# Batched matrix product on one core: two groups stored between loads, the rest in three transfers, and eight blocks of the last half copied by VectorE

## The chip, the core and the metric

The kernel runs on one core of one Trainium2 chip. The metric is the device time of one execution in microseconds; before the change it was 132.04 us, the median of three runs (131.92 to 132.06). The engines named below are TensorE (PE, with its weight loads as PEld), VectorE (DVE), ScalarE (ACT), GpSimd (POOL) and SyncE (SP), which here computes nothing and issues all transfers.

## What is computed

```python
def setup_inputs():
    batch, dim_i, dim_j, dim_k = 32, 256, 512, 384
    return {
        "x": np.random.randn(batch, dim_i, dim_j).astype(np.float32),
        "y": np.random.randn(batch, dim_j, dim_k).astype(np.float32),
    }

def reference(x: np.ndarray, y: np.ndarray) -> np.ndarray:
    return np.einsum('bij,bjk->bik', x, y).astype(np.float32)
```

These are 32 products of a 256 x 512 matrix with a 512 x 384 matrix in float32. Read from DRAM are 41.94 MB, written are 12.58 MB.

## The kernel before

The 32 batches are cut into N = 8 groups of Q = 4. Each batch of a group has a quarter of the 128 partitions (PQ = 32). A group's x is one load of 2048 KB, its y one load of 3072 KB; x and y each have two buffers, so group n uses the buffers of group n − 2. The result of every group has its own place in `o_sb`, which holds the whole output, 1536 KB for each group; no store has to be finished before a buffer can be used again.

A group is worked in two halves (NE = 2, the loop over `e`), each with half of the rows of x. For each group GpSimd rounds x to float16 (`round_x`, one cast for each half) and y (`round_y`, two casts of 128 x 3072, or four of 128 x 1536 in groups 0, 6 and 7). VectorE transposes x in blocks of 32 x 32, four pieces for each half (`transpose_x`). TensorE makes 64 small products for each half, in four chunks of 16 (NC = 4); a chunk waits for its piece of y and of transposed x. The products add up in the PSUM banks of the half; two halves have different banks.

A half's result is 16 blocks of 32 x 384 (`BLOCKS`, in order of bank g and row block h). They are copied from PSUM to `o_sb` by two engines: the last five (`OWN = 5`) by VectorE, at the end of `vector_half`, the other eleven by ScalarE, in `scalar_half`, which waits for each bank in turn. In the last half of the last group VectorE first waits until all of its matmuls are done, and then copies its five; it has no more transposes by then. Both engines raise a semaphore at the end of each half (`s_act`, `s_dve`). TensorE takes one from each before a half starts. So when the first chunk of a group's second half is done, both halves of the group before it have been copied. The stores rest on that.

SyncE's program sets the order of all transfers. Ahead of it stand the loads of groups 0 and 1 (y, x, x, y). Then, for n from 2 to 7, x of group n is issued when GpSimd has rounded both halves of x of group n − 2, and y of group n when the first half of x of group n − 1 is rounded, which GpSimd does only after y of group n − 2. The first store, of groups 0 to 5 (`JOINED = 6`), is issued behind all loads, when the first chunk of the second half of group 6 is done. The second, of groups 6 and 7, is issued when the copies of the last half are finished. SyncE then waits for both to land. All of these transfers go through one queue, in the order in which they are issued, spread over the 16 DMA engines. In DRAM and in `o_sb`, each partition's part of a group is one run of 12,288 bytes, whatever number of groups a store has.

Names for the steps below: `chunk_done(n, e, a)` is the count of `s_pe` at which chunk a of half e of group n is done; `s_cast` counts the rounded halves of x; `store(first, last)` is one transfer of the groups from `first` up to, but without, `last`.

Of the kernel before, what the change touches and what calls it, by code (L numbers as in the profile page):

```python
# [11 lines left out]
Q = 4  # L12
NE = 2
STEP = 4
STRAIGHT = 2
JOINED = 6


@with_exitstack
def kernel(  # L20
# [13 lines left out]
    H = R // NE  # L34
    T = J // PQ
    TW = T // 2
    N = B // Q
# [20 lines left out]
    s_act = nc.alloc_semaphore("s_act")  # L58
    s_dve = nc.alloc_semaphore("s_dve")
    s_pe = nc.alloc_semaphore("s_pe")  # L60
    s_sp = nc.alloc_semaphore("s_sp")
    s_out = nc.alloc_semaphore("s_out")
    mine = s_x + s_y + [s_xt, s_yr, s_cast, s_free, s_act, s_dve, s_pe, s_sp]
# [3 lines left out]
    def load_x(n):  # L67
        src = x[n * Q : (n + 1) * Q].rearrange("g (p r) j -> (g p) r j", r=R)
        return nc.sync.dma_start(out=x_sb[n % 2], in_=src).then_inc(s_x[n], 16)

    def load_y(n):
        src = y[n * Q : (n + 1) * Q].rearrange("g (q t) k -> (g q) t k", t=T)
        return nc.sync.dma_start(out=y_sb[n % 2], in_=src).then_inc(s_y[n], 16)
# [11 lines left out]
    def bank_done(n, e, g):  # L85
        return (n * NE + e) * MARKS + NC + g

    def chunk_done(n, e, a):
        return (n * NE + e) * MARKS + (a + 1 if a < NC - 1 else MARKS)

    sp = nc.sync

    def store(first, last):
        groups = out[first * Q : last * Q].rearrange("(n g) (s f) k -> (g s) n f k", g=Q, s=PQ)
        src = o_sb[:, first:last].rearrange("p n e h k -> p n (e h) k")
        sp.dma_start(out=groups, in_=src).then_inc(s_out, 16)

    for n in range(2, N):
        sp.wait_ge(s_cast, NE * (n - 1))
        load_x(n)  # L100
        sp.wait_ge(s_cast, NE * (n - 1) + 1)
        load_y(n)
    sp.wait_ge(s_pe, chunk_done(JOINED, NE - 1, 0))
    store(0, JOINED)
    sp.wait_ge(s_pe, chunk_done(N - 1, NE - 1, 0))
    sp.drain()
    sp.wait_ge(s_act, NE)
    sp.wait_ge(s_dve, NE)
    store(JOINED, N)
    sp.sem_inc(s_sp, 1)  # L110
    sp.wait_op(s_out, 16 * 2, "sem-ge").then_inc(s_out, -16 * 2)

# [34 lines left out]
    v = nc.vector  # L149
# [4 lines left out]
    def transpose_x(e, a):  # L154
        w = slice(a * AW, (a + 1) * AW)
        v.transpose(xt_w[:, w], words[:, e, w]).then_inc(s_xt, 1)  # L156

    BLOCKS = [(g, h) for g in range(Q) for h in range(H)]  # L160
    OWN = 5

    def collect(copy, n, e, blocks, first=None, last=None):
        for i, (g, h) in enumerate(blocks):
            ins = copy(  # L165
                o_sb[g * PQ : (g + 1) * PQ, n, e, h],
                o_ps[h * PQ : (h + 1) * PQ, e * Q + g, :K],
            )
            if i == 0 and first is not None:
                ins.then_inc(first, 1)  # L170
            if i == len(blocks) - 1 and last is not None:
                ins.then_inc(last, 1)

    def vector_half(n, e):
        for a in range(NC):
# [3 lines left out]
            transpose_x(1 - e, a)  # L179
        collect(v.tensor_copy, n, e, BLOCKS[-OWN:], s_free, s_dve)  # L180

# [6 lines left out]
            vector_half(n, e)  # L188
    vector_half(N - 1, 0)
    v.wait_ge(s_pe, chunk_done(N - 1, 1, NC - 1))  # L190
    collect(v.tensor_copy, N - 1, 1, BLOCKS[-OWN:], None, s_dve)

    a_ = nc.scalar

    def scalar_half(n, e):
        for g in range(Q - 1):
            a_.wait_ge(s_pe, bank_done(n, e, g))
            blocks = [b for b in BLOCKS[:-OWN] if b[0] == g]
            collect(a_.copy, n, e, blocks, None, s_act if g == Q - 2 else None)


    a_.copy(spare, nc.const_aps.tensor(0.0, [1, 1], F32))  # L202
    a_.sem_inc(s_act, NE)
    with a_.Fori(0, N - STRAIGHT) as n:
        with a_.Fori(0, NE) as e:
            scalar_half(n, e)
    for n in range(N - STRAIGHT, N):
        for e in range(NE):
            scalar_half(n, e)

    te = nc.tensor

# [68 lines left out]
```

## Time and profile before

| | |
|---|---|
| median of 3 runs | 132.04 us |
| the profiled execution, its own time | 132.04 us |
| its span (first to last instruction) | 130.7 us |
| outside the span | 1.34 us |
| granted TensorE clock, mean | 0.831 |
| TensorE matmul busy | 64.1 us (49%) |
| VectorE busy | 82.5 us (63%) |
| ScalarE busy | 84.3 us (64%) |
| GpSimd busy | 74.1 us (57%) |
| moved by DMA | 54.55 MB, mean 417 GB/s |

All times of the profile are in microseconds from the start of the span, unless marked ns. A row of the timeline has the start, the duration, the engine, the line, the operation with its output and input, and how many instructions of the kind were merged into the row; in brackets stands how long the engine was idle before, and who ended that. A row of a transfer has the output and input, the issuing queue, the count, the size and the time from issue to landing; where one issue is wanted, the view was limited to a window that holds it alone. A row of the windows has the stretch, its length, the busy time and the count for PE, PEld, DVE, ACT and POOL, then the granted TensorE clock, the busy share of the 16 DMA engines, and GB/s.

### The profile page before, as it was taken

The page shows a single profiled execution, that of the slowest core. Times are in us where ns is not written, and L with a number is a line of the kernel's source. Part 1 is how long each engine was busy: PE and PEld are TensorE (multiplying, and loading weights), DVE is VectorE, ACT ScalarE, POOL GpSimd, SP SyncE. Part 2 cuts the span into 40 slices and gives each one's busy share as a digit, 9 for nine tenths or more (in the row PEclk, how much of TensorE's full clock was granted, in tenths as well). Part 3 has the DMA queues.
Part 4 walks back from the last instruction along what each step waited for, and adds up shares of the span by engine and source line. Part 5 has one row for each costly group of instructions (what it writes and reads, how often), then busy time and mean ns, then how long its engine had stood idle before and what let it go on. Part 6 is the DMA issues. An engine that isn't in the chain of part 4 may idle for free. (4 is left out here: it accounts for less than half of the span.)

```text
span 130.7 us, 3199 instructions
## 1 busy us (share of the span) xinstructions
PE 64.1 (49%) x1024; PEld 48.7 (37%) x1024; DVE 82.5 (63%) x144; ACT 84.3 (64%) x178; POOL 74.1 (57%) x42
## 2 busy tenths in 40 slices
PE   0000009950797199369909945892684498100000
PEld 0000009930796086169805524761252255000000
DVE  0000036599549998996999799899979959900000
ACT  0400000399809997996999699899989958993000
POOL 0006991089946993995599399757973970000000
PEclk9999999999559959955896897799999869955555
DMA  5999999999999999999999999999999999999995
GB/s 128 451 399 451 411 451 429 466 399 446 414 434 406 456 421 416 441 439 429 431 444 399 451 406 469 399 416 436 474 399 400 432 427 429 440 425 421 432 432 244
DMA packets 3363, 54.55 MB, mean 417 GB/s; under 512 B 288, under 2 KB 288, under 8 KB 288
## 3 DMA queue, kind: packets, MB, share of 16 engines
q1 hardware_dynamic: 3360, 54.53, 98.1%
q14 instruction: 3, 0.02, 0.0%
HBM read 41.94 MB, written 12.58 MB: 417 GB/s over the span
## 5 line engine op out<-in xcount | busy, mean ns | idle before, releaser
L165 ACT COPY o_sb<-o_ps (+1 forms) x176 | 82.8, 470 | 30.9 <-PE o_ps L217 28.8
L217 PE MATMUL o_ps<-y_r,xt_sb 32*128 32x384 f16 x1024 | 64.1, 393 | 47.6 <-PEq L214 47.5
L217 PEld LDWEIGHTS o_ps<-y_r,xt_sb 32*128 32x128 f16 x1024 | 48.7, 110 | 62.6 <-issue 54.4
L156 DVE STREAM_TRANSPOSE xt_sb<-x_r 128x256 f32<-128x256 f32 x64 | 37.9, 624 | 30.5 <-POOL x_r L126 18.4
L136 POOL CAST y_r<-y_sb 128x1536 f16<-128x1536 f32 (+1 forms) x22 | 44.3, 2050 | 13.8 <-DMA y_sb<-in_y_dram 13.8
L165 DVE COPY o_sb<-o_ps 32x384 f32 (+1 forms) x80 | 44.6, 557 | 1.6
L126 POOL CAST x_r<-x_sb 128x2048 f16<-128x2048 f32 x16 | 30.2, 1896 | 18.9 <-DVE o_sb L165 16.0
L202 ACT ACT_TABLE_LOAD x1 | 1.3, 1283 | 3.5 <-PEq L78 3.5
L265 POOL MEMSET const-float32-0.0<- 128x1 f32 x1 | 0.1, 98 | 0.2 <-issue 0.2
L202 ACT COPY spare<-const-float32-0.0 1x1 f32<-1x1 f32 x1 | 0.2, 190 | 0.0
L265 POOL MEMSET const-uint8-127<- 128x1 uint8 x1 | 0.1, 102 | 0.0
L265 POOL MEMSET const-bfloat16-1.0<- 128x1 bf16 x1 | 0.1, 101 | 0.0
L265 POOL MEMSET const-float32-1.0<- 128x1 f32 x1 | 0.1, 99 | 0.0
## 6 DMA issues: line engine op xcount, KB each, us to landing
y_sb<-in_y_dram SPq DMA_DIRECT2D x8, 3072.0 KB, 15.5
x_sb<-in_x_dram SPq DMA_DIRECT2D x8, 2048.0 KB, 15.4
out_dram<-o_sb SPq DMA_DIRECT2D x1, 9216.0 KB, 26.0
out_dram<-o_sb SPq DMA_DIRECT2D x1, 3072.0 KB, 12.0
```

Of the source, the lines that this page charges most:

```text
L126: po.tensor_copy(x_r[:, e], x_sb[n % 2][:, e * H : (e + 1) * H]).then_inc(s_cast, 1)
L136: ins = po.tensor_copy(y_r[:, s], y_sb[n % 2][:, s])
L156: v.transpose(xt_w[:, w], words[:, e, w]).then_inc(s_xt, 1)
L165: ins = copy(o_sb[g * PQ : (g + 1) * PQ, n, e, h], o_ps[h * PQ : (h + 1) * PQ, e * Q + g, :K],)
L202: a_.copy(spare, nc.const_aps.tensor(0.0, [1, 1], F32))
L217: return te.add_instruction(mybir.InstMatmult(name=nc.get_next_instruction_name(), start_tensor_calc=start, stop_tensor_calc=stop, tile_si ...
L265: nc = _bacc.Bacc("TRN2", target_bir_lowering=False, num_devices=1)
```

## The change

SyncE issues the store of groups 0 and 1 between the loads of x and y of group 5 (`BEHIND = 5`), behind a wait for the first chunk of the second half of group 2. The rest of the output goes in three transfers in place of two: groups 2 to 5, where the store of groups 0 to 5 was; group 6, when the first chunk of the second half of group 7 is done; and group 7, when the last copies are finished. The drain of SyncE ahead of the last waits is gone, and the final wait counts four stores.

In the last half of the last group, VectorE copies the last 8 of the 16 blocks (`LAST_OWN = 2 * H`, H = 4) and ScalarE the first 8, those of banks 0 and 1. All other halves stay at 5 and 11.

```diff
+EARLY = 2
+BEHIND = 5
 JOINED = 6
...
     for n in range(2, N):
         sp.wait_ge(s_cast, NE * (n - 1))
         load_x(n)
+        if n == BEHIND:
+            sp.wait_ge(s_pe, chunk_done(EARLY, NE - 1, 0))
+            store(0, EARLY)
         sp.wait_ge(s_cast, NE * (n - 1) + 1)
         load_y(n)
     sp.wait_ge(s_pe, chunk_done(JOINED, NE - 1, 0))
-    store(0, JOINED)
+    store(EARLY, JOINED)
     sp.wait_ge(s_pe, chunk_done(N - 1, NE - 1, 0))
-    sp.drain()
+    store(JOINED, N - 1)
     sp.wait_ge(s_act, NE)
     sp.wait_ge(s_dve, NE)
-    store(JOINED, N)
+    store(N - 1, N)
     sp.sem_inc(s_sp, 1)
-    sp.wait_op(s_out, 16 * 2, "sem-ge").then_inc(s_out, -16 * 2)
+    sp.wait_op(s_out, 16 * 4, "sem-ge").then_inc(s_out, -16 * 4)
...
     OWN = 5
+    LAST_OWN = 2 * H
...
-    collect(v.tensor_copy, N - 1, 1, BLOCKS[-OWN:], None, s_dve)
+    collect(v.tensor_copy, N - 1, 1, BLOCKS[-LAST_OWN:], None, s_dve)
...
-    def scalar_half(n, e):
-        for g in range(Q - 1):
+    def scalar_half(n, e, own=OWN):
+        mine = BLOCKS[:-own]
+        for g in range(mine[-1][0] + 1):
             a_.wait_ge(s_pe, bank_done(n, e, g))
-            blocks = [b for b in BLOCKS[:-OWN] if b[0] == g]
-            collect(a_.copy, n, e, blocks, None, s_act if g == Q - 2 else None)
+            blocks = [b for b in mine if b[0] == g]
+            collect(a_.copy, n, e, blocks, None, s_act if g == mine[-1][0] else None)
...
-            scalar_half(n, e)
+            scalar_half(n, e, LAST_OWN if (n, e) == (N - 1, NE - 1) else OWN)
```

## Prediction

> **What bounds the kernel now.** I read the page first, then SyncE's order of issues, then how long each transfer took to land, then the last 30 us.
>
> ```profile
> span 130.7 us, 3199 instructions
> ...
> DMA  5999999999999999999999999999999999999995
> ...
> q1 hardware_dynamic: 3360, 54.53, 98.1%
> ...
> ACT o_sb L165 8%; PE o_ps L217 4%
> ```
>
> The second row is the mean busy share of the 16 DMA engines in 40 slices: nine tenths or more in every slice but the first and the last. The third row is the one queue through which all loads and stores go: 54.53 MB, and its packets take 98.1% of the span of 16 engines. The last row is the chain of waits; it covers only 12% of the span, and ends in ScalarE's copies, after which only the last store is left. So the bound is the bytes in the queue, and the kernel can lose or gain only where the queue stands empty, or where a transfer has a price beside its bytes. The bytes are the same before and after.
>
> SyncE's issues (start, duration, line, count):
>
> ```profile
> 0.74 0.39 SPq L73 DMA_DIRECT2D y_sb<-in_y_dram  x1
> ...
> 53.42 0.33 SPq L69 DMA_DIRECT2D x_sb<-in_x_dram  x1
> 60.65 0.33 SPq L73 DMA_DIRECT2D y_sb<-in_y_dram  x1
> ...
> 76.85 0.33 SPq L69 DMA_DIRECT2D x_sb<-in_x_dram  x1
> 84.08 0.33 SPq L73 DMA_DIRECT2D y_sb<-in_y_dram  x1
> 97.43 21.69 SPq L96 DMA_DIRECT2D out_dram<-o_sb  x2
> ```
>
> These are y of group 0, x and y of group 5, x and y of group 7, and the two stores (97.43, and the second at 118.72, quoted below). From issue to landing, in the same order, for y of group 0, x and y of group 7 and the stores of six groups and of two:
>
> ```profile
> y_sb<-in_y_dram SPq DMA_DIRECT2D x1, 3072.0 KB, 10.1
> x_sb<-in_x_dram SPq DMA_DIRECT2D x1, 2048.0 KB, 16.9
> y_sb<-in_y_dram SPq DMA_DIRECT2D x1, 3072.0 KB, 17.1
> out_dram<-o_sb SPq DMA_DIRECT2D x1, 9216.0 KB, 26.0
> out_dram<-o_sb SPq DMA_DIRECT2D x1, 3072.0 KB, 12.0
> ```
>
> Issue plus this time gives the landings: x of group 7 at 93.75, its y at 101.18, the first store at 123.43, the second at 130.72, which is the end of the span. The second store was issued 4.7 us before the first one had landed, so it waited in the queue and never let it run dry: it landed 7.29 us behind the first. **7.3 us is what two groups' store costs in a full queue**, 3.65 us for one group.
>
> **The store of groups 0 and 1.** Its wait is for the first chunk of the second half of group 2.
>
> ```profile
> 50.31 2.78 PEld L217 LDWEIGHTS o_ps<-y_r,xt_sb 32*128 32x128 f16 x64 [0.53 <-issue]
> ...
> 76.78 5.44 POOL L136 CAST y_r<-y_sb 128x3072 f16<-128x3072 f32 x2
> ...
> 82.16 1.90 POOL L126 CAST x_r<-x_sb 128x2048 f16<-128x2048 f32 x1
> ```
>
> TensorE loads the 64 weights of that half from 50.31 on, in four chunks, so the first chunk is over around 51; SyncE comes to the wait at 53.42 + 0.33 = 53.75 and finds it met. Queued behind it on SyncE is y of group 5, which is issued at 60.65 in any case, since it waits for a cast: nothing is late there, and the added 0.4 us of issuing is hidden in that wait (were the cover gone, it would delay y by those 0.4 us, in a queue that holds over 10 us of work).
>
> In the queue the store stands ahead of y of group 5. That y, and all transfers behind it, land 7.3 us later. Does the queue run dry later for that? The issue most at risk is y of group 7, which waits for GpSimd's cast of x of group 6, behind the cast of y of group 5. That cast of y begins at 76.78 now, right when y lands, and at 84.1 then; it takes 5.44, the x cast 1.90, so y of group 7 is issued at 91.4. x of group 7 ahead of it lands at 93.75 + 7.3 = 101.05. The cover is 9.7 us. The queue stays full, and all work from group 5 on is 7.3 us later: y of group 7 lands at 108.5. The price of the store is the time that it no longer takes at the end: zero in the sum.
>
> **Two more transfers, two more turns.** There are four stores for two, and the queue turns once more from reading DRAM to writing it, and once from writing to reading. The first store's 9216 KB took 123.43 − 101.18 = 22.25 us, against 3 × 7.29 = 21.87 for three times the second store, which has three transfers' worth of fixed cost in it: a boundary in a full queue shows no price. The 0.38 us over may be a turn to writing, or engines that end at different times. Bounds: nothing below (no byte is saved), 0.38 for a turn to writing. A turn from writing to reading has no row; its ends are nothing and the price of a load that finds the queue empty. That was paid by y of group 0: with its first packets at 1.75 (row below) it landed at 10.84, 9.09 us for 3072 KB against 7.29, so 1.8 us. The rows nearest to a turn in a full queue are those of stores behind loads, so I take **0.2 us for all of it** and keep 0 to 2.2.
>
> The Trainium skill, in "DMA: Bandwidth & Descriptors", section "Anatomy of one DMA — SWDGE (gpsimd) path", speaks against this change: every DMA has a fixed cost of about 2.0 us whatever its size, most of it for confirming the last write. Two more in series would be 4 us by that. The rows agree for a transfer that finds the queue empty (1.8 us), and not for one in a full queue.
>
> **The tail.** Copies of the last group (start, duration, engine, count), the matmuls of its halves, and the last issue:
>
> ```profile
> 103.21 4.87 PE L217 MATMUL o_ps<-y_r,xt_sb 32*128 32x384 f16 x64 [3.87 <-PEq L214]
> ...
> 108.10 10.60 ACT L165 COPY o_sb<-o_ps 32x384 f32<-32x384 f32 x22 [1.74 <-PE o_ps L217]
> ...
> 108.48 3.21 PE L217 MATMUL o_ps<-y_r,xt_sb 32*128 32x384 f16 x64 [0.40 <-PEq L214]
> 108.86 5.73 DVE L165 COPY o_sb<-o_ps 32x384 f32<-32x384 f32 x10
> 118.72 0.39 SPq L96 DMA_DIRECT2D out_dram<-o_sb  x1
> ```
>
> ScalarE makes 22 copies in 10.60 us, 0.482 each, and ends at 118.70; VectorE makes 10 in 5.73, 0.573 each. With 8 blocks each in the last half, ScalarE makes 11 + 8 = 19 copies and ends at 108.10 + 9.16 = 117.26. VectorE ends its first five at 111.73, just behind the last matmul (111.69), and eight more at 116.31. ScalarE is still the later, and the last store can be issued 1.44 us earlier: at 118.72 − 1.44 + 7.3 = **124.58**. Before, these 1.44 us would have been hidden, for the queue was full until 123.43; now they count. Without them the issue would be at 126.02.
>
> When does the queue run dry? Quarters of a microsecond, DMA share and GB/s at the end of the row; a packet counts where it starts:
>
> ```profile
> 1.75:2.00 0.25, 0.00 (x0) 0.00 (x0) 0.00 (x0) 0.00 (x0) 0.00 (x0) 1.00 4.66 1081
> ...
> 128.75:129.00 0.25, 0.00 (x0) 0.00 (x0) 0.00 (x0) 0.00 (x0) 0.00 (x0) 0.50 1.27 541
> ...
> 129.75:130.00 0.25, 0.00 (x0) 0.00 (x0) 0.00 (x0) 0.00 (x0) 0.00 (x0) 0.50 0.12 49
> ```
>
> The first engines start their last packet before 129.0, the last one at 129.75 or later: they end raggedly, over about 1 us. One group's store earlier, and with the 0.2 us, they run out of group 6's store from about 125.5 on. The last store's packets start about 1.0 us behind its issue (0.74 to 1.75 for the first load): 125.6. The two meet. If the queue is never dry, the span is 130.7 + 0.2 = 130.9. If the store starts cold, it ends at 124.58 + 1.0 + 3.65 + 1.8 = 131.05. The later one holds: **131.05**, or 0.35 over the span before. The two issues of 0.39 us ahead of it (groups 2 to 5, and 6) are made while SyncE waits for the copies, and the removed drain is worth nothing that a row shows.
>
> The sum: 0 for the moved store, 0.2 for boundaries and turns, 0.15 for the cold start beside them; with the 1.34 us that lie outside the span (132.04 less 130.7) the profiled execution becomes 132.39. It equals the median of the runs shown, so I forecast **132.4 us**. About 0.2%, or 0.26 us, is what a measurement here can tell from no change.
>
> **Rivals.** (a) *Nothing shows, the not-slower side*: boundaries and turns cost nothing and the last store arrives in time: 132.0 to 132.2. For it: no boundary shows a price in the rows. It decides as soon as the store is issued about 0.2 us earlier, or a store's start, which reads on-chip memory, costs less than the first load's 1.8.
>
> (b) *The tail is late.* TensorE's clock (the number ahead of the DMA share) changes within the last group:
>
> ```profile
> 106.00:107.00 1.00, 1.00 (x17) 0.55 (x9) 0.64 (x1) 0.36 (x1) 0.96 (x1) 0.50 1.03 426
> 107.00:108.00 1.00, 1.00 (x21) 0.39 (x16) 0.55 (x1) 0.00 (x0) 0.00 (x0) 0.94 1.04 442
> ```
>
> Its first half ran mostly at half clock (4.87 us), the second at full (3.21). Shifted by 7.3 us, the second half can fall in a stretch at half clock and take 1.66 us more; VectorE, which waits for all of it, would start at 113.35 and end at 117.93, past ScalarE's 117.26, and a slow last chunk of the first half adds some 0.4. The store is then up to 1.1 us later, and so is the end: 132.8 to 133.5. A first half at full clock gains little, as the casts feed it. (c) *A turn from writing to reading costs like a cold load*, 1.8 us, and everything behind it, the last store too, moves: 131.05 + 1.8 + 1.34 = 134.2. Against it: the next loads already stand in the queue. (d) *Each added transfer pays its price in series*, 2 × 1.8: 135.6; the second store's 7.29 us speaks against it. (e) *Faster*: the ragged end shrinks, as the last transfer is half as long, and the engines end together near 129.5 instead of past 130: 131.5. No row shows a reason.
>
> **How the numbers follow.** Forecast 0.38, (a) 0.30, (b) 0.16, (c) 0.06, (d) 0.02, (e) 0.08. The range from 131.8 to 133.4 holds the forecast, (a), nearly all of (b) and a part of (e). The forecast lies 0.36 over the time before, just past what can be told apart, so 0.31 of its 0.38 count as slower; with (b), (c) and (d) that makes 0.55. Same: 0.07 of it and most of (a), 0.36. Faster: 0.09.
>
> **What would show it.** y of group 5 landing 7.3 us later, near 84; y of group 7 issued near 91 and the queue still full then; y of group 7 landing near 108.5, where later means a turn's price; ScalarE's last run with 19 copies; the last issue near 124.6, and whether the DMA share dips around 125.5. A dip of over 1 us makes (b), none makes (a). A queue that is empty anywhere between 60 and 108 would make the argument wrong.

## The result, and the profile after

| | before | after |
|---|---|---|
| median | 132.06 us (6 runs, 131.92 to 132.14) | 133.23 us (6 runs, 132.96 to 133.34) |
| ratio, with its 95% interval | | 1.0086 (1.0073 to 1.0099) |
| the profiled execution, its own time | 132.04 us | 133.21 us |
| its span | 130.7 us | 131.8 us |

The change makes the kernel 1.17 us slower. From the page after:

```profile
span 131.8 us, 3200 instructions
...
DMA  5999999999999999998999999999999999999994
...
q1 hardware_dynamic: 3392, 54.53, 97.6%
...
ACT o_sb L172 7%; PE o_ps L225 1%
```

The bytes are the same, and the 16 DMA engines are as busy as before in nearly every slice. 97.6% of 131.8 is 128.6 us of packets, against 98.1% of 130.7 = 128.2 before: the mean engine works 0.4 us longer for the same bytes, and the span is 1.1 us longer. SyncE's issues after, and then the landings of y of group 0, the early store, y of groups 5 and 7, the store of groups 2 to 5 and the last store, each from its issue:

```profile
53.78 0.33 SPq L71 DMA_DIRECT2D x_sb<-in_x_dram  x1
54.16 0.43 SPq L98 DMA_DIRECT2D out_dram<-o_sb  x1
61.01 0.34 SPq L75 DMA_DIRECT2D y_sb<-in_y_dram  x1
...
77.22 0.33 SPq L71 DMA_DIRECT2D x_sb<-in_x_dram  x1
92.03 0.33 SPq L75 DMA_DIRECT2D y_sb<-in_y_dram  x1
106.19 19.36 SPq L98 DMA_DIRECT2D out_dram<-o_sb  x3
```

```profile
y_sb<-in_y_dram SPq DMA_DIRECT2D x1, 3072.0 KB, 10.4
out_dram<-o_sb SPq DMA_DIRECT2D x1, 3072.0 KB, 23.2
y_sb<-in_y_dram SPq DMA_DIRECT2D x1, 3072.0 KB, 23.6
y_sb<-in_y_dram SPq DMA_DIRECT2D x1, 3072.0 KB, 17.1
out_dram<-o_sb SPq DMA_DIRECT2D x1, 6144.0 KB, 18.2
out_dram<-o_sb SPq DMA_DIRECT2D x1, 1536.0 KB, 6.6
```

The early store is issued right behind x of group 5, without a wait, and lands at 77.36; y of group 5 lands at 84.61, y of group 7 at 109.13 (101.18 before), groups 2 to 5 at 124.39. The last issue ends at 106.19 + 19.36 = 125.55, so it begins at 125.16, and lands 6.6 us later, at 131.8. The tail's timeline after:

```profile
111.11 3.87 PE L225 MATMUL o_ps<-y_r,xt_sb 32*128 32x384 f16 x48 [3.00 <-PEq L222]
...
116.03 9.16 ACT L172 COPY o_sb<-o_ps 32x384 f32<-32x384 f32 x19 [1.11 <-PE o_ps L225]
...
116.46 3.17 PE L225 MATMUL o_ps<-y_r,xt_sb 32*128 32x384 f16 x64 [0.43 <-PEq L222]
116.80 7.42 DVE L172 COPY o_sb<-o_ps 32x384 f32<-32x384 f32 x13
```

The copies stand as in the sum: 19 in 9.16 us on ScalarE, which ends at 125.19, and VectorE before it, at 124.22. How the engines end, by the share of all 16 that is busy (second last column), in the kernel before and then after:

```profile
129.00:130.00 1.00, 0.00 (x0) 0.00 (x0) 0.00 (x0) 0.00 (x0) 0.00 (x0) 0.50 0.27 111
130.00:130.70 0.70, 0.00 (x0) 0.00 (x0) 0.00 (x0) 0.00 (x0) 0.00 (x0) 0.50 0.00 0
```

```profile
129.00:130.00 1.00, 0.00 (x0) 0.00 (x0) 0.00 (x0) 0.00 (x0) 0.00 (x0) 0.50 0.87 369
130.00:131.80 1.80, 0.00 (x0) 0.00 (x0) 0.00 (x0) 0.00 (x0) 0.00 (x0) 0.50 0.07 27
```

In the last 1.8 us after, a share of 0.07 is 2.0 us of work, about what one engine does. The trace has 16 landings for each transfer, one for each engine's part, and the end is the last of them: here fifteen parts of the last store landed from 130.14 to 131.10, and the sixteenth at 131.81. The page's busy share, a mean of 16, does not show that one.

### The profile page after: what moved, and what is told of

The parts are those of the page before. It is cut to its first block, busy times and chain, and to the rows that moved or that the text cites. A ratio compares the mean times of both kernels' runs of the same rounds, so it can differ in the third digit from the quotient of the medians.

```text
span 131.8 us, 3200 instructions
## 1 busy us (share of the span) xinstructions
PE 65.6 (50%) x1024; PEld 53.1 (40%) x1024; DVE 84.1 (64%) x147; ACT 82.8 (63%) x175; POOL 74.1 (56%) x42
## 3 DMA queue, kind: packets, MB, share of 16 engines
q1 hardware_dynamic: 3392, 54.53, 97.6%
## 5 line engine op out<-in xcount | busy, mean ns | idle before, releaser
L172 ACT COPY o_sb<-o_ps (+1 forms) x173 | 81.4, 470 | 38.7 <-PE o_ps L225 36.7
L225 PE MATMUL o_ps<-y_r,xt_sb 32*128 32x384 f16 x1024 | 65.6, 407 | 54.0 <-PEq L222 50.6
L225 PEld LDWEIGHTS o_ps<-y_r,xt_sb 32*128 32x128 f16 x1024 | 53.1, 113 | 66.2 <-issue 59.3
L172 DVE COPY o_sb<-o_ps 32x384 f32 (+1 forms) x83 | 46.2, 557 | 1.7
```

The source lines that it names most:

```text
L172: ins = copy(o_sb[g * PQ : (g + 1) * PQ, n, e, h], o_ps[h * PQ : (h + 1) * PQ, e * Q + g, :K],)
L225: return te.add_instruction(mybir.InstMatmult(name=nc.get_next_instruction_name(), start_tensor_calc=start, stop_tensor_calc=stop, tile_si ...
```

## The experiments

Two things were read from the trace's packet records in every run. A store's packet of 12,288 bytes takes 460 ns where nothing disturbs it. The records do not name the engine; packets of which each starts where the one before it ends are taken for one engine's. In the kernel before, there is such a run of some 16 packets, with 484 to 549 ns each, beside the matmuls of the last group. And in most kernels with an early store there is a stretch of 2 to 3 us in which loads' packets on all 16 engines take longer. The table has, for each profiled execution: the sum of what the slow store packets of one engine (about 478 ns and more) take over 460 ns, ahead of the last load (early) and beside group 7's matmuls or later (late), the time that slow loads cost per engine (their excess over 912 or 611 ns, divided by 16), the mean and the last of the 16 landings of the last transfer, all in us. Packets of under 12 KB are not in its first two columns, nor are those slowed by more than 180 ns that start where an instruction load of 8 KB ends (in the kernel before, one of 698 ns at 100.89, where a load begun at 100.58 had taken 309 ns). As engines are told apart by times alone, the late column is good to about 0.1 us.

```
kernel            early  late  loads  mean end  last end   time of this execution
before             0     0.79  0       129.86    130.68    132.04
before_again       0     0.79  0       129.87    130.44    131.84
no_early           0     0.89  0.01    129.88    130.49    131.85
tiny_early         0     0.79  0.13    129.90    130.74    132.13
pe_on              0     2.48  0       129.97    132.31    133.68
one_before_x       0     0.86  0.44    130.26    131.04    132.44
one_early          0.33  0.78  0.39    130.19    131.42    132.82
four_turns         -     0.81  0.50    130.28    131.26    132.62
four_together      -     0.87  0.41    130.56    131.52    132.89
store_before_x     0.36  0.84  0.44    130.89    131.53    132.89
two_gaps           0.02  0.87  0.56    131.13    131.34    132.70
after              0.84  0.80  0.44    130.56    131.81    133.21
after_again        0.73  0.85  0.38    130.41    131.70    133.10
own5_last          0.84  0.77  0.53    132.12    132.19    133.56
```

The late column is some 0.8 us in every kernel but `pe_on`, with an early store or without.

Three theories stood at the start: the last store meets a drained queue (1), the turns between loads and stores and the further transfers cost (2), and the engine that ends last carries delays of its own (3). The expectations below add two: 3a, matmuls slow one engine's stores, and 4, having an early store at all is what costs.

**Parts of the change alone.** `no_early` takes the early store out:

```diff
-        if n == BEHIND:
-            sp.wait_ge(s_pe, chunk_done(EARLY, NE - 1, 0))
-            store(0, EARLY)
...
-    store(EARLY, JOINED)
+    store(0, JOINED)
```

> The early store is taken out; groups 0 to 5, 6 and 7 go in three transfers at the end, and VectorE copies 8 of the last 16 blocks. Theory 1: the last copies are done near 117.3 and the queue is full until about 127, so 132.0 to 132.2. Theory 2: one boundary more than before and no turn back to reading, so 132.0 to 132.3. Theory 3: 132.0 to 133.0, by how late the first load lands and what hits the last engine.

Measured: 132.00 us, ratio to before 0.9998 (0.9982 to 1.0014). The split of the end, one transfer more, VectorE's eight blocks and the missing drain neither cost nor save together, within that interval of about 0.2 us. The 1.17 us come with the early store.

`one_early` stores only group 0 there, with `EARLY = 1`:

> Only group 0 is stored between x and y of group 5; groups 1 to 5, 6 and 7 in three transfers at the end. The last copies are then 3.65 us earlier against the same end of the queue, so the last store finds the queue full. Dry queue at the end (theory 1): nearly all of the 1.17 us is gone, 132.1 to 132.4. Turn between stores and loads, and the number of transfers (theory 2): the turns and transfers are the same as in the changed kernel, so it stays at 132.9 to 133.3. Slowest engine (theory 3: the engines start and end raggedly, and the one that ends last carries delays from the start and from other packets on it, which differ from program to program): anywhere between 132.0 and 133.2, with a first load that lands later than 10.84 us in step with the time.

Measured: 132.62 us, 1.0037 (1.0019 to 1.0056), about half of the loss for half of the bytes. That is above what a drained queue alone would leave and below what turns would. It lies in the wide range of theory 3, but the sign named there failed: the first load's landing did not follow the time (10.98 us for the last of its 16 parts, 11.14 in the changed kernel, 10.99 in `before_again`).

`own5_last` gives ScalarE its 11 blocks back:

```diff
-    LAST_OWN = 2 * H
+    LAST_OWN = OWN
```

> The changed kernel, but VectorE copies 5 of the last 16 blocks again and ScalarE 11. The last issue is 1.44 us later, near 126.6. Theory 1: the queue is already drained at the last store, so the end moves by the full 1.4 us, to 134.5 to 134.8. Theories 2 and 3: the last store still had some cover on the engine that ends last; the end moves by less, 133.6 to 134.3.

Measured: 133.51 us, 1.0103 (1.0066 to 1.0139), some 0.2 to 0.3 us above the changed kernel, where the drained queue wanted 1.4, and 0.1 below the least that the other theories had expected. So the drained queue is not what the changed kernel pays. The last column but one of the table says how: here all engines end within 0.07 us of their mean (132.12 and 132.19). The last issue, 106.01 + 21.47 − 0.39 = 127.09, is 1.93 us later than in the changed kernel, and the end 0.38: the slowest engine had some 1.5 us of older work left in the changed kernel's execution.

```profile
106.01 21.47 SPq L98 DMA_DIRECT2D out_dram<-o_sb  x3
```

`before_again` is the kernel before, unchanged:

> The kernel before, unchanged, for a second profile: by all theories 132.0 to 132.2. Under theory 3 the landing of the first load and the ragged end may differ from the first profile's 10.84 and 0.9 us, and the time with them.

Measured: 131.84 us. Its first load lands at 10.99, later than the 10.79 of the first profile by the same event, and its time is shorter: in this pair, how raggedly the engines start is not what sets the time.

**Matmuls beside stores.** `pe_on` is the kernel before, with matmuls added that compute nothing for the output:

```diff
+    te.wait_ge(s_act, 1)
+    te.wait_ge(s_dve, 1)
+    with te.Fori(0, 20):
+        for t in range(4):
+            for g in range(Q):
+                s = slice(g * PQ, (g + 1) * PQ)
+                product(o_ps[:, g, K:512], xt[s, t // 2, :, t % 2], y_r[s, t, :512 - K], True, True, g)
+    product(o_ps[:, 0, K:512], xt[:PQ, 0, :, 0], y_r[:PQ, 0, :512 - K], True, True, 0).then_inc(s_pe, 1)
```

> The kernel before, with 321 more small matmuls (128 columns each, into unused columns of PSUM, read by nothing) behind the last half, so that TensorE goes on working while the last stores run. In the packet records of before, one of the 16 DMA engines takes 484 to 549 ns for each of 16 packets in a row where the others take 460, and that stretch (103.8 to 111.8) is the one in which TensorE works on the last group. If stores that run beside matmuls are slowed on one engine (theory 3a), that engine goes on losing some 45 ns a packet for 20 to 30 packets more: 132.6 to 133.5. If turns and transfers, or a drained queue, are the cost (theories 1 and 2): 131.9 to 132.2.

Measured: 133.43 us, 1.0106 (1.0089 to 1.0123). The only wait for them stands on SyncE behind the last store's issue, and they end at 122.87, long before that store lands; the queue has the same transfers. From its timeline and its windows:

```profile
113.91 8.96 PE L218 MATMUL o_ps<-y_r,xt_sb 32*128 32x128 f16 x321 [2.24 <-ACT o_sb L166]
```

```profile
103.20:112.00 8.80, 8.27 (x128) 4.22 (x128) 6.41 (x12) 6.42 (x15) 3.75 (x3) 0.81 1.01 427
112.00:113.90 1.90, 0.00 (x0) 0.02 (x1) 1.83 (x5) 1.84 (x5) 0.00 (x0) 1.00 0.98 420
113.90:123.00 9.10, 8.50 (x321) 5.61 (x321) 1.10 (x2) 5.07 (x11) 0.00 (x0) 0.81 1.01 427
123.00:129.00 6.00, 0.00 (x0) 0.00 (x0) 0.00 (x0) 0.00 (x0) 0.00 (x0) 0.68 1.00 428
129.00:130.00 1.00, 0.00 (x0) 0.00 (x0) 0.00 (x0) 0.00 (x0) 0.00 (x0) 0.50 0.32 135
130.00:132.30 2.30, 0.00 (x0) 0.00 (x0) 0.00 (x0) 0.00 (x0) 0.00 (x0) 0.50 0.05 21
```

Fifteen engines are done by 130.35, much as before; 0.05 of 16 engines over 2.3 us is 1.8 us of one engine that works on alone. The slow packets' start and duration (us, ns), beside them:

```
103.85 512  104.35 501  104.85 493  105.34 512  106.30 507  107.28 493  107.76 502  108.26 521
108.78 484  109.26 521  109.78 531  110.31 559  110.85 521  111.37 512
114.17 568  114.74 578  115.31 540  115.85 578  116.41 578  116.98 568  117.53 568  118.09 568
118.65 596  119.24 578  119.81 540  120.35 531  120.88 587  121.46 568  122.02 549  122.57 568  123.13 493
```

They stop where TensorE pauses (111.9 to 113.9), though VectorE and ScalarE go on copying there, and where it ends. That TensorE's work slows the stores of one DMA engine is shown: the slow stretch came and went with the matmuls, and the end moved with it. How it does so is not shown. The loads that ran beside matmuls earlier in the same trace have no such packets.

`store_before_x`, `one_before_x` and `two_gaps` move early stores into TensorE's pauses. The first puts the changed kernel's early store ahead of x of group 5:

```diff
-        load_x(n)
         if n == BEHIND:
             sp.wait_ge(s_pe, chunk_done(EARLY, NE - 1, 0))
             store(0, EARLY)
+        load_x(n)
```

> The changed kernel, with the early store ahead of x of group 5 in place of behind it, so that about half of it runs where TensorE is idle between groups 3 and 4. Theory 3a (matmuls beside a store slow one engine): the delay of that engine halves, 132.6 to 133.0. Theory 2 (turns): the same turns, 133.1 to 133.4. Theory 1 (drained queue): the end of the queue and the last copies stand as in the changed kernel, 133.1 to 133.4.

Measured: 132.86 us, 1.0059 (1.0043 to 1.0076). The slow engine's early part fell from 0.84 to 0.36 us (0.73 in `after_again`), and the time by 0.37, as the theory of the matmuls has it; the intervals of the two ratios only just meet. Here the mean engine did wait for the last store (it landed 4.18 us behind the one before, where a full queue takes 3.65), but the last engine did not (131.53 − 127.88 = 3.65).

`one_before_x` does the same with `EARLY = 1`:

> Only group 0 is stored early, ahead of x of group 5, in TensorE's pause. one_early, where it stands behind that x and beside matmuls, had 132.62. Theory 3a: only a stall of all engines once in the run, 0.2 to 0.4 us, remains: 132.2 to 132.45. Without an effect of matmuls: 132.5 to 132.7, as one_early.

Measured: 132.62 us, 1.0045 (1.0004 to 1.0087), four runs from 132.27 to 133.51, as spread as the runs of before beside them (131.74 to 132.78). By its time alone it tells nothing apart. By its packets it does: none of the early store's is slow (0 against 0.33 us in `one_early`), and the last engine of the profiled execution ends 0.38 us earlier.

`two_gaps` stores groups 0 and 1 one by one, each in a pause:

```diff
-        load_x(n)
-        if n == BEHIND:
+        if BEHIND <= n < BEHIND + EARLY:
             sp.wait_ge(s_pe, chunk_done(EARLY, NE - 1, 0))
-            store(0, EARLY)
+            store(n - BEHIND, n - BEHIND + 1)
+        load_x(n)
```

> Groups 0 and 1 are both stored early, as in the changed kernel, but one ahead of x of group 5 and one ahead of x of group 6, where each falls mostly into TensorE's pause between two groups. One transfer and one turn more than the changed kernel, the same bytes early, the same end. Theory 3a (matmuls slow one engine's stores): that engine loses little beside the early stores, and the time falls by 0.5 to 0.8 us, to 132.4 to 132.8. Theory 2 (turns): 133.3 to 133.6. Theory 1 (drained queue): 133.1 to 133.4.

Measured: 133.08 us, 1.0073 (1.0040 to 1.0106), six runs from 132.70 to 133.77; the changed kernel beside it (`after_again`) had 133.06. The expected gain of 0.5 to 0.8 us did not come. The slow packets are gone (0.02 us early), and yet the end hardly moved, for here another limit was next: its last transfer lands 4.41 us behind the one before it in the mean of the 16 engines, where a full queue takes 3.65, so most engines stood empty and waited for the last store, and all end within 0.21 us of their mean.

```profile
105.86 20.61 SPq L98 DMA_DIRECT2D out_dram<-o_sb  x3
```

```profile
129.00:130.00 1.00, 0.00 (x0) 0.00 (x0) 0.00 (x0) 0.00 (x0) 0.00 (x0) 0.50 0.95 406
130.00:131.40 1.40, 0.00 (x0) 0.00 (x0) 0.00 (x0) 0.00 (x0) 0.00 (x0) 0.50 0.36 149
```

In this kernel the drained queue does count. Its last issue, at 105.86 + 20.61 − 0.39 = 126.08, is 0.92 us later than in the changed kernel. One part of that is the prediction's rival (b): from 114 to 116 us TensorE was still granted a clock of 0.50 here, where the changed kernel had 0.86 and 1.00. The profiled execution was the quickest of the six; what the others lost is not known.

**Turns and transfers.** `four_turns` stores group 0 in quarters behind x of groups 4 to 7, with `EARLY = 1`, `PARTS = 4` and `FP = R // PARTS`; `four_together` issues all four behind x of group 5. The diff is that of `four_turns`:

```diff
+    def store_part(i):
+        rows = out[0:Q].rearrange("g (s f) k -> (g s) f k", s=PQ)[:, i * FP : (i + 1) * FP]
+        src = o_sb[:, 0].rearrange("p e h k -> p (e h) k")[:, i * FP : (i + 1) * FP]
+        sp.dma_start(out=rows, in_=src).then_inc(s_out, 16)
...
-        if n == BEHIND:
+        if n >= N - PARTS:
             sp.wait_ge(s_pe, chunk_done(EARLY, NE - 1, 0))
-            store(0, EARLY)
+            store_part(n - (N - PARTS))
```

> Only group 0 is stored early, in four parts of 384 KB, behind x of groups 4, 5, 6 and 7: four turns where one_early had one, for the same bytes. Theory 2: one_early's 0.6 us were its turn, so four turns give 133.5 to 134.5. Theory 3a: the same bytes beside matmuls, 132.4 to 132.9.

Measured: 132.59 us, 1.0045 (1.0028 to 1.0062): four turns cost no more than `one_early`'s one. Only ahead of the first of them are the loads slow.

> Group 0 in the same four parts, all four between x and y of group 5: one turn, three transfers more than one_early. If a transfer in a full queue has a price of its own, 0.1 us each: 132.9; if not: 132.5 to 132.7 by both theories 2 and 3a. It is the control for four_turns.

Measured: 133.02 us, 1.0086 (1.0069 to 1.0103), 0.4 us above `one_early`, for three more transfers in a row and packets a quarter as long. That is a price of 0.1 us each, though `no_early`, with one more transfer of 12,288-byte packets, paid none; transfers and short packets were not separated. Part of it may be matmuls again: the short packets, 121 ns undisturbed, took up to 215 ns beside them, 0.64 us in all (0.16 in `four_turns`), and not on one engine alone.

`tiny_early` stores a part of group 0 behind x of group 5, and the rest at the end. The part is one of R = 8 rows in each partition, an eighth of the group, in packets of 1,536 bytes:

```diff
-            sp.wait_ge(s_pe, chunk_done(EARLY, NE - 1, 0))
-            store(0, EARLY)
+            sp.wait_ge(s_pe, chunk_done(1, NE - 1, 0))
+            store_part(0, 1)
...
-    store(EARLY, JOINED)
+    store_part(1, R)
+    store(1, JOINED)
```

> A quarter of group 0 (384 KB) is stored early, behind x of group 5; the other three quarters and groups 1 to 5, 6 and 7 go at the end, in four transfers. The traces with early stores each have a stretch in which the packets of all 16 engines take longer and the landings fall back by 0.2 to 0.5 us for good. If that belongs to having an early store at all (theory 4), it stays: 132.2 to 132.5. If it goes with the bytes stored early: 132.0 to 132.15.

That is half of what its expectation names: 192 KB, not 384 KB. Measured: 131.94 us, 0.9985 (0.9951 to 1.0018): no loss that can be told apart. Having an early store, with its turn back to reading, is not what costs 1.17 us.

**The changed kernel once more.**

> The changed kernel once more, on the chip of the three above, for a second profile. 133.1 to 133.4 by all theories. Theory 3a: again one engine has some 15 slow packets beside group 4's matmuls and some 15 beside group 7's, and the last landing stands 1.2 us or more behind the mean of its 16. Theory 4: again one stretch with slow packets on all engines.

Measured: 133.06 us, 1.0070 (1.0036 to 1.0103). Again one engine has slow packets beside group 4's matmuls (13, 0.73 us) and beside group 7's, the last landing is 1.29 us behind the mean, and there is one stretch of slow loads on all engines. It lies in another place, though: at 66 to 68 us, just ahead of the early store's packets, where the first profile had it at 31 to 34. The windows that hold them, first 25 to 39 us before and after, then 58 to 68 us before and in `after_again`:

```profile
25.00:39.00 14.00, 8.44 (x136) 7.87 (x131) 10.35 (x18) 10.37 (x23) 10.95 (x5) 0.76 1.00 427
```

```profile
25.00:39.00 14.00, 8.39 (x135) 7.89 (x131) 10.34 (x18) 10.35 (x22) 10.95 (x5) 0.76 0.99 415
```

```profile
58.00:68.00 10.00, 7.15 (x117) 6.51 (x109) 8.37 (x15) 8.49 (x19) 7.04 (x4) 0.76 0.98 421
```

```profile
58.00:68.00 10.00, 5.34 (x97) 3.08 (x96) 7.99 (x14) 7.72 (x18) 6.97 (x5) 0.84 0.98 404
```

The share stays at full, since slow packets count as busy; only the last column shows the loss: 12 GB/s over 14 us, or 17 over 10, is 0.17 MB, which is 0.4 us at 427 GB/s. A busy share alone would have hidden it.

## Why the prediction was right in sign, and what its sum missed

The forecast was 132.4 us, 0.36 over the time before; measured was 1.17 over. The range held the time, and slower was the likelier side, but the sum had the wrong terms in it. That the range held was luck: its upper part stood there for rival (b), a late tail, which did not occur in the changed kernel.

- **The bound, and the moved store's place in the queue: right.** No wait at 54.16, y of group 5 issued at 61.01 as if nothing stood before it, y of group 7 at 92.03 (91.4 in the sum), with x of group 7 landing at 101.7 and the queue full.
- **"The price of the store is the time that it no longer takes at the end: zero in the sum". This step failed.** It took the queue for one server whose work only changes places. It is 16 engines, and the end is the last one's. Stored beside group 4's matmuls, the moved bytes cost one engine 0.84 us (0.73 in the second profile). At the end nothing is saved for it: the stores beside group 7's matmuls have their slow packets as before (0.80 us, 0.79 before), and what became shorter there is only the part behind them, where TensorE has stopped and hardly a packet is slow. That both delays fall on the same engine is read from the landings: the last part of group 6's store lands 1.35 us behind the mean of its 16 in the changed kernel, and 0.61 in `no_early`. `pe_on` shows the cause, and `store_before_x` that the cost shrinks with the overlap.
- **"0.2 us for all of it" (boundaries and turns): mis-sized, and not a price by the turn.** The loads lost 0.44 us per engine in the changed kernel and 0.38 in its second profile. It is not a price for each turn or transfer: four turns had 0.50, one 0.39, an eighth of a group 0.13, and one more transfer at the end none. In the changed kernel most of it came at 31 to 34 us, before any store. y of group 7 landed 0.6 us late, which the prediction would have read as a turn's price. 0.44 and 0.84 are 1.28 us, beside 131.81 − 130.68 = 1.13 from last landing to last landing; 0.38 and 0.73 for `after_again` are 1.11, beside 1.02; 0.39 and 0.33 for `one_early` are 0.72, beside 0.74. The fit can be no closer: the loads' part is a mean of 16 engines and not the slow engine's own loss, and the last landings of the kernel before differ by 0.24 between its two profiles. For `two_gaps`, and for `four_turns` and `four_together`, whose short packets are not counted, this sum falls short, by 0.4 us in `four_together`.
- **The cold start of the last store, 0.15: not paid by the engine that ends last.** The last engine's landing stands 3.64 us behind its one before, as in a full queue (3.65); the mean engine lost 0.08. The last issue came at 125.16 rather than 124.58, 0.58 later, since y of group 7 landed 0.6 us later; it still was early enough for the slowest engine. The sum read the ragged end, and then let the first engines to run dry set the time.
- **VectorE's eight blocks: the copies exactly as worked out, their worth not.** 1.44 us of earlier copies are worth 0.2 to 0.3 us in the changed kernel, as the slowest engine still had work.
- **Rivals.** (a), nothing shows, is what `no_early` and `tiny_early` do, not the change; the sign named for it, no dip of the DMA share near 125.5, did appear (0.93 from 125 to 126) and pointed wrong, since that share is a mean. (b), a late tail by the clock, did not come: the last half ran at full clock (3.17 us), and the queue, not the copies, set the end. (c), 1.8 us for a turn back to reading, did not come either: `four_turns` has four such turns and is 0.6 us over the kernel before. (d), a price for each added transfer in series, is not paid at the end of the queue: `no_early` makes one transfer more than before, at 0.9998 of its time. The Trainium skill, "DMA: Bandwidth & Descriptors", section "Anatomy of one DMA — SWDGE (gpsimd) path", gives a fixed cost of about 2 us for a DMA that GpSimd issues; the transfers here are issued by SyncE, and that run shows no such cost in its time. (e), engines that end more together, was the wrong way round: the last landing is 1.25 us behind the mean, where it was 0.82.

**What stays open** is the stretch of slow loads. All nine profiles in which group 0 or more is stored early lose 0.38 to 0.56 us to it, `tiny_early` 0.13, the four without an early store 0.01 or nothing. Mostly it lies 2 to 3 us ahead of the first early packet, but twice (`after`, and `four_together`) the larger part came at 31 to 34 us, over 20 us ahead of the early store's issue. No run here tells why, so this part of the 1.17 us goes with the early store in these profiles and is not explained.

No version that was run beats the kernel before: `tiny_early` and `no_early` tie with it.

## What to carry to other kernels

Where the DMA queue is full from end to end, ask what ends last among its 16 engines rather than how busy they are in the mean: the shares of the last microseconds show it (0.05 of 16 engines for 2.3 us is one engine alone). Moving bytes in a full queue is not free when it changes what they run beside: here the stores lost least where TensorE was silent. And a second limit close behind the first (the last copies, some 1.5 us away) takes the gain when the first is mended, as `two_gaps` shows.

## What was not expected of the hardware

In these traces TensorE's work slows the stores, and only those, of one of the 16 DMA engines. Beside the last group of the kernel before, 128 matmuls and 128 weight loads cost that engine 0.79 us, or 3.1 ns an instruction; in `pe_on`, 321 and 321 cost 1.75 us, 2.7 ns each. By columns it would be 16 ps (0.79 us over 128 x 384) against 43 (1.75 over 321 x 128): the cost goes with the instructions, not with the columns that the matmuls stream. Matmuls and weight loads come in equal numbers in both, and each weight load has the same size, so which of the two it is stays open. Whether it is the instructions themselves or the profiler's recording of them was not tried, and every run whose packets were read was recorded, so what a run without recording pays is not known.
